# A hybrid encoder block with product-key experts: half of the last products in float32r parts, one load ahead, one load tied, the accumulator in four pieces

## The chip, the core and the metric

The kernel runs on one core of one Trainium2 chip. Its five engines are named as in the profile: PE (matrix products; PEld is its loading of weights), DVE (vector), ACT (scalar, activation functions), POOL, and SP, which here only issues DMA transfers. The metric is the device time of one execution in microseconds (us).

## The reference

`x` is 512 tokens by 1024 features in float32. One layer is computed:

```python
h = rms_norm(x, norm1_g)
q, k, v, xr, yr, gate_logits = split(h @ w_in)
attn = diff_attention(q, k, v, ...)            # 8 heads, two softmaxes each, chunk-causal
rnn = rg_lru(conv(xr), ...) * gelu(yr)         # 1280 channels
merged = sigmoid(g_A) * (attn @ P_A) + sigmoid(g_R) * (rnn @ P_R)
x = x + merged @ w_out
h = rms_norm(x, norm2_g)
# PEER: per token 8 heads pick 16 of 16384 experts each, by product keys
act = gelu(sum_d u_tab[idx] * h)               # 128 chosen rows per token
x = x + sum_k softmax(score) * act * v_tab[idx]
```

`u_tab` and `v_tab` are 16384 by 1024 in float32.

## The kernel before, in words

Tokens lie in four blocks of 128. Block 0 goes through everything up to the keys as pass 0, blocks 1 to 3 as pass 1. The experts are then computed in two ways. For blocks 0 and 1 each token's rows are gathered (`experts`, L843): 128 slots per block, in each slot an indirect DMA of POOL (L871) fetches 1 MB, a row of `u` and of `v` for each token, into one of four buffers `uv`; DVE multiplies and sums the `u` half with `h` (L883 for block 0, L857 for block 1), ACT makes the weight from it (L862, L863), and DVE adds the weighted `v` half to the output (L848).

Blocks 2 and 3 together (256 tokens) go through all experts (`dense`, L995). The tables are cut into 128 chunks of 128 experts. Each chunk c has an "up" product, `u` chunk times `h` into PSUM tile `pup` or `st`, then a gelu by ACT into `y` (L946), and a "down" product, which adds `o` times `v` chunk to an accumulator `acc` in PSUM of 256 tokens by 1024 features, held over all 128 chunks. `o` is `y` times the tokens' weights for these experts (L1060, DVE). The weights are built before (`wbuild`, L1011), written to a DRAM tensor `w_d` in 16 groups of tokens, and read back as tiles `w` for 12 chunks each (L1048).

47 up products are made ahead. The other 81 (`up_near`) are made between the down products, from chunk 32 on: each has its `u` chunk loaded as `raw`, cast by ACT to float32r (L926), and the rest of the cast taken by DVE (L927); the two parts are the tile `t`. Such a product with both factors in parts is three float32r products, high by high, high by low and low by high (`mm`, L207). A down product is plain float32: 4 calls of 128x128 by 128x512, each of which the profile shows as two MATMUL instructions, so 8 in all.

The slots of block 1 (`second`, L1125) are let go step by step beside the dense part: 0.6 of a slot for each down product alone, 1.1 where an up product goes with it (`share`).

Every engine takes its instructions in one order, which a scheduler sets when the kernel is built. A `v` load brings two chunks (1 MB). `v` and `t` tiles share four buffers of 8 KB, `raw` has three, `o` three. SP issues the loads in its own order, and one that waits holds back those behind it. `tc.add_manual_dep(..., in_turn)` ties an instruction behind another.

The change touches the head (L117, L395 to L398), `dense` (L997, L1000, the tie at L1048 and L1056, the down product L1050 to L1065) and its end (L1091 to L1095).

Of the kernel before, what the change touches and what calls it, by code (L numbers as in the profile page):

```python
# [10 lines left out]
F32 = mybir.dt.float32  # L11
F32R = mybir.dt.float32r
# [51 lines left out]
def block_kernel(  # L64
# [23 lines left out]
    uvp = ctx.enter_context(tc.tile_pool(name="uvp", bufs=4))  # L88
# [3 lines left out]
    wp = ctx.enter_context(tc.tile_pool(name="wp", bufs=4))  # L92
    rg = ctx.enter_context(tc.tile_pool(name="rg", bufs=5))
# [97 lines left out]
    x1_d = dram.tile([3, P, D], F32, name="x1_d")  # L191
# [7 lines left out]
    def rstd_of(ss, w, scale):  # L199
        xx = small(w)  # L200
        nc.gpsimd.tensor_scalar(xx, ss, scale, EPS, op0=ALU.mult, op1=ALU.add)  # L201
        y = small(w)
        nc.gpsimd.tensor_tensor(y, xx, mhalf[:, 0:w], op=ALU.pow)
        return y


    def mm(o, lhs, rhs, start, stop):  # L207
        terms = [(0, 0)] if len(lhs) == 1 or len(rhs) == 1 else [(0, 0), (0, 1), (1, 0)]
        made = [
            nc.tensor.matmul(  # L210
                o, lhs[a], rhs[b], start=start and i == 0, stop=stop and i == len(terms) - 1
            )
            for i, (a, b) in enumerate(terms)
        ]
        return made[0]


    in_turn = mybir.DependencyInfo(mybir.DependencyClass.Sync, mybir.DependencyReason.SCHED_ONLY)
# [129 lines left out]
    class Pass:  # L348
# [43 lines left out]
            return [h[:, k, :] for h in self.hT]  # L392


        def head(self):  # L395
            nb, NT = self.nb, self.NT
            xt = self.region([P, nb, D])
            nc.sync.dma_start(xt, x[self.t0 : self.t0 + NT, :].rearrange("(b p) d -> p b d", p=P))  # L398
            self.hT = self.parts()
            for b in range(nb):  # L400
                hh = s4.tile([P, D], F32, tag="s4", name=nm("hh"))
                ss = small(1)
                A.activation(hh, xt[:, b, :], AF.Square, accum_out=ss)  # L403
                rs = rstd_of(ss, 1, 1.0 / D)
                A.activation(hh, xt[:, b, :], AF.Copy, scale=rs[:, 0:1])
                for k in range(0, KT, 4):
                    pt = psum("pth")
                    for j in range(4):
                        nc.tensor.transpose(pt[:, j * P : (j + 1) * P], hh[:, (k + j) * P : (k + j + 1) * P], ident)
                    for j in range(4):  # L410
                        g1 = cst[:, C_N1 + k + j : C_N1 + k + j + 1]
                        o = self.hT[0][:, k + j, b * P : (b + 1) * P]
                        pj = pt[:, j * P : (j + 1) * P]
                        A.activation(o, pj, AF.Copy, scale=g1)
                        if self.split:
                            V.scalar_tensor_tensor(
                                self.hT[1][:, k + j, b * P : (b + 1) * P], pj, g1, o.bitcast(F32),
                                op0=ALU.mult, op1=ALU.subtract,
                            )
# [484 lines left out]
    NT2 = 2 * P  # L904
    TG = 16
    NG = NT2 // TG
    NCH = SLOTS
# [8 lines left out]

    WI = 12

    w_d = dram.tile([NG, P, NCH, TG], F32, name="w_d")

    def chunk(src, c, name):
# [41 lines left out]
    turn, owed = [None], [0.0]  # L963
    SHARE = {"far": 0.2, "w": 0.5, "down": 0.6, "both": 1.1}

    def share(step):
        owed[0] += SHARE[step]
        while owed[0] >= 1:
            owed[0] -= 1
            next(ex, None)  # L970
# [23 lines left out]

    def dense(ys, kT, kTb, stack):  # L995
        pool = lambda n, bufs=1, **kw: stack.enter_context(tc.tile_pool(name=n, bufs=bufs, reuse_waits="tile", **kw))
        dw = pool("dw")  # L997
        pa = pool("pa", space=PSUM)
        pt_ = pool("pt", 2, space=PSUM)
        acc = pa.tile([P, 2, D], F32, tag="acc", name="acc")  # L1000

        def up_near(after=None):
            c = TURN[len(ys)]
# [35 lines left out]
        ws, vs = [], []  # L1039

        def wtile():
            n = min(WI, NCH - len(ws) * WI)
            ws.append(rg.tile([P, NG, n, TG], F32, tag="r", name=nm("w")))

        def wload(j, g0=0, g1=NG):
            i1, w = j * WI, ws[j]
            n = w.shape[2]
            nc.sync.dma_start(w[:, g0:g1], w_d[g0:g1, :, i1 : i1 + n, :].rearrange("g p i t -> p g i t"))  # L1048

        def down(c, y):  # L1050
            if c % WI == 0 and len(ws) * WI < NCH:
                wtile()
                wload(len(ws) - 1)
            if c % 2 == 0:
                vs.append(wp.tile([P, 2, D], F32, tag="w8", name=nm("v")))
                nc.sync.dma_start(vs[-1], v_t[c : c + 2].rearrange("c p d -> p c d"))  # L1056
            v_ = vs[-1][:, c % 2, :]
            o = mid.tile([P, NT2], F32, tag="o", name=nm("o"), bufs=OB)
            yv = y.rearrange("p (g t) -> p g t", g=NG)
            turn[0] = V.tensor_mul(o.rearrange("p (g t) -> p g t", g=NG), yv, ws[c // WI][:, :, c % WI, :])  # L1060
            for b in range(2):
                bs = slice(b * P, (b + 1) * P)
                for hf in range(2):
                    hs = slice(hf * 512, hf * 512 + 512)
                    mm(acc[:, b, hs], [o[:, bs]], [v_[:, hs]], c == 0, c == NCH - 1)  # L1065

        for tg in range(NG):
            last = wbuild(tg)
# [6 lines left out]
                wload(0, 0, 8)  # L1075
            elif tg == 13:
                wload(0, 8, 14)
        wload(0, 14, NG)
        while len(ys) < AHEAD:
            up_near(last)  # L1080

        A.copy(h2s[0], p1.h2r)
        V.tensor_tensor(h2s[1], p1.h2r, h2s[0].bitcast(F32), op=ALU.subtract)
        for c in range(NCH):
            down(c, ys[c])

            more = c >= HEAD + SPARE and len(ys) < NCH
            if more:
                up_near()
            share("both" if more else "down")  # L1090
        for b in range(2):  # L1091
            ob = wp.tile([P, D], F32, tag="raw", name=nm("ob"), bufs=3)
            nc.sync.dma_start(ob, x1_d[1 + b])
            V.tensor_add(ob, ob, acc[:, b, :])
            nc.sync.dma_start(out[(2 + b) * P : (3 + b) * P, :], ob)  # L1095

    p0, p1 = Pass(0, 1, False), Pass(1, 3, True)
    st = {}
    p0.head()
    run(p0.qkv(0, st))  # L1100
    attend(p0, st)
    run(p0.rnn())
# [37 lines left out]
    with ExitStack() as stack:  # L1140
        dense(ys, *kTs, stack)
# [83 lines left out]
```

## Time and profile before

| | |
|---|---|
| median of 3 runs | 1873.72 us (1872.7 to 1874.15) |
| the profiled execution's own time | 1872.16 us |
| its span, first to last instruction | 1870.4 us |
| mean granted TensorE clock | 0.956 of full speed |
| busy, PE / PEld / DVE / ACT / POOL | 93% / 73% / 70% / 42% / 27% of the span |
| chain that ended last | PE 73%, DMA 10%, DVE 8%, ACT 4%, issue 4%, POOL 2% |
| read from HBM, written | 539.68 MB, 22.02 MB (300 GB/s over the span) |

How to read it: times in the trace are counted from the span's start. A stretch given as A:B is from A to B us. "DMA share" is the mean busy share of the core's 16 DMA engines. Matmuls are pipelined and their ends modelled, so the mean duration of one overlaps its neighbours; the time that a run of them takes is read from the chain. The granted clock is 1.00 where PE runs at 2.4 GHz. The dense part's down products lie from about 1185 to 1864 us.

### The profile page before, as it was taken

How to read it: one execution, taken by the hardware profiler on the slowest of the kernel's cores; microseconds unless marked ns; L12 is line 12 of the kernel's file. 1: busy time of each engine (PE TensorE's matmuls, PEld its weight loads, DVE VectorE, ACT ScalarE, POOL GpSimd, SP SyncE). 2: the span in 40 equal slices, each digit the busy share in tenths (PEclk: the TensorE clock that was granted, in tenths of full speed). 3: DMA queues.
4: the chain of work that ended last, by engine and by line, in shares of the span. 5: the costliest groups of instructions: out<-in, count | busy, mean ns of one | idle time of the engine just before them, and what ended most of it. 6: DMA issues, size and time to landing. Idle time of an engine off the chain costs nothing.

```text
span 1870.4 us, 25606 instructions
## 1 busy us (share of the span) xinstructions
PE 1739.8 (93%) x9102; PEld 1366.9 (73%) x9102; DVE 1303.3 (70%) x2811; ACT 780.0 (42%) x2188; POOL 498.4 (27%) x375
## 2 busy tenths in 40 slices
PE   7899898889969899998999987899999999999998
PEld 6689797778849677778988976444767667766763
DVE  2251287999999987679999787345766666766663
ACT  3382334676678754345411576001222233222220
POOL 1100001544342233332000477121322232222220
PEclk9899898889869899998999999999999999999999
DMA  7478554887878899988566677999999999999894
GB/s 302 146 273 312 187 184 158 301 310 259 328 274 306 325 360 360 380 313 304 169 195 222 207 273 304 365 389 341 401 358 377 380 370 371 342 363 361 336 357 186
DMA packets 131471, 563.37 MB, mean 301 GB/s; under 512 B 11408, under 2 KB 43280, under 8 KB 88592
## 3 DMA queue, kind: packets, MB, share of 16 engines
q1 hardware_dynamic: 94480, 293.29, 43.2%
q0 software_dynamic: 36864, 268.45, 38.1%
q8 instruction: 72, 1.18, 0.2%
q14 instruction: 55, 0.45, 0.1%
HBM read 539.68 MB, written 22.02 MB: 300 GB/s over the span
## 4 chain that ended last, share of the span: by engine, by line
PE 73%; DMA 10%; DVE 8%; ACT 4%; issue 4%; POOL 2%; DVEq 0%; SPq 0%; POOLq 0%; ACTq 0%
PE acc L210 22%; PE st L210 15%; PE pup L210 5%; PE ppq L210 5%; DMA uv<-in_uv_dram,idx 5%; PE pgt L210 4%; PE pkq L210 4%; PE pbR L690 4%; PE pbA L683 3%; PE pwo L717 3%; DMA v<-in_v_t_dram 2%; DVE x1f L848 2%; PE pvv L210 2%; PE pw L1034 1%; DVE uv L883 1%
## 5 line engine op out<-in xcount | busy, mean ns | idle before, releaser
L871 POOL DMA_INDIRECT uv<-in_uv_dram,idx x256 | 362.7, 1417 | 1074.1 <-DVE x1g L848 265.5
L210 PE MATMUL acc<-v,o 128*128 128x512 f32 x1024 | 448.8, 594 | 4.4 <-DMA v<-in_v_t_dram 4.4
L210 PEld LDWEIGHTS acc<-v,o 128*128 128x128 f32 x1024 | 191.8, 190 | 230.1 <-issue 223.3
L210 PE MATMUL st<-h2s,t 128*128 128x256 f32 x1944 | 252.6, 288 | 0.0
L210 PEld LDWEIGHTS st<-h2s,t 128*128 128x128 f32 x1944 | 235.0, 188 | 20.1 <-issue 17.2
L848 DVE SCALAR_TENSOR_TENSOR x1g<-uv,e,x1g 128x1024 f32<-128x1024 f32 x128 | 164.3, 1284 | 47.5 <-ACT e L863 47.4
L848 DVE SCALAR_TENSOR_TENSOR x1f<-uv,e,x1f 128x1024 f32<-128x1024 f32 x128 | 163.7, 1279 | 18.4 <-ACT e L894 18.3
L883 DVE SCALAR_TENSOR_TENSOR uv<-uv,h2f 128x1024 f32<-128x1024 f32 x128 | 155.6, 1217 | 29.3 <-DMA uv<-in_uv_dram,idx 28.3
L862 ACT ACTIVATE e<-e 128x1 f32<-128x1 f32 x128 | 25.9, 202 | 335.9 <-DVE uv L857 335.2
L857 DVE SCALAR_TENSOR_TENSOR uv<-uv,h2g 128x1024 f32<-128x1024 f32 x128 | 156.4, 1222 | 10.7 <-DMA uv<-in_uv_dram,idx 5.7
L927 DVE TENSOR_TENSOR t<-raw,t 128x1024 fp32r<-128x1024 f32 x81 | 99.0, 1222 | 69.3 <-ACT t L926 69.3
L210 PE MATMUL pup<-r,u 128*128 128x256 f32 x496 | 107.6, 379 | 0.3 <-DMA u<-in_u_t_dram 0.3
L234 DVE TENSOR_TENSOR wl<-raw,wh 128x1024 fp32r<-128x1024 f32 x76 | 90.9, 1217 | 21.1 <-PE pgt L210 10.1
L946 ACT ACTIVATE y<-st 128x256 f32<-128x256 f32 x81 | 31.1, 384 | 176.1 <-PE st L210 176.1
L210 PEld LDWEIGHTS pup<-r,u 128*128 128x128 f32 x496 | 93.9, 190 | 13.4 <-issue 0.8
L1060 DVE TENSOR_TENSOR o<-y,w 128x256 f32<-128x256 f32 x96 | 40.6, 423 | 90.3 <-PE acc L210 90.1
L926 ACT CAST t<-raw 128x1024 fp32r<-128x1024 f32 x81 | 83.8, 1034 | 23.4 <-PE acc L210 23.4
L233 ACT CAST wh<-raw 128x1024 fp32r<-128x1024 f32 x76 | 76.7, 1044 | 30.1 <-PE pwo L717 11.2
L1034 PE MATMUL pw<-o1s,o 128*128 128x128 f32 x512 | 66.8, 285 | 18.8 <-ACT wst L1035 8.9
L1033 POOL TENSOR_SCALAR o1s<-iota,r 128x128 f32<-128x128 bf16 x64 | 80.5, 1266 | 10.0 <-issue 4.2
L1034 PEld LDWEIGHTS pw<-o1s,o 128*128 128x128 f32 x512 | 62.6, 196 | 23.4 <-ACT wst L1035 10.5
L201 POOL TENSOR_SCALAR sm<-sm 128x1 f32<-128x1 f32 (+4 forms) x24 | 9.6, 398 | 253.6 <-ACT hh L403 111.5
(271 smaller groups left out, 3340.6 us busy)
## 6 DMA issues: line engine op xcount, KB each, us to landing
v<-in_v_t_dram SPq DMA_DIRECT2D x64, 1024.0 KB, 9.2
raw<-in_u_t_dram SPq DMA_DIRECT2D x81, 512.0 KB, 8.7
u<-in_u_t_dram SPq DMA_DIRECT2D x47, 512.0 KB, 4.0
w<-in_w_br_dram SPq DMA_DIRECT2D x16, 1024.0 KB, 5.0
w_d<-wst SPq DMA_DIRECT2D x16, 1024.0 KB, 5.1
w<-w_d SPq DMA_DIRECT2D x9, 1536.0 KB, 14.0
w<-in_w_qkv_dram SPq DMA_DIRECT2D x12, 1024.0 KB, 6.8
raw<-in_w_qkv_dram SPq DMA_DIRECT2D x24, 512.0 KB, 6.2
```

The lines of the kernel that those rows point to most:

```text
L210: nc.tensor.matmul(o, lhs[a], rhs[b], start=start and i == 0, stop=stop and i == len(terms) - 1)
L233: A.copy(hi[:, i : i + 1024], raw)
L234: V.tensor_tensor(lo[:, i : i + 1024], raw, hi[:, i : i + 1024].bitcast(F32), op=ALU.subtract)
L690: nc.tensor.matmul(pb[:, 0:NT], w.raw(1024 + k * P, 1024 + (k + 1) * P), self.rnn_out(k, 1)[:, 0, :], start=(k == 0), stop=(k == NF - 1),)
L848: V.scalar_tensor_tensor(x1, v_, e_, x1, op0=ALU.mult, op1=ALU.add)
L857: i = V.scalar_tensor_tensor(t[:, 0:D], t[:, 0:D], 1.0, h2, op0=ALU.mult, op1=ALU.mult, accum_out=d)
L871: i = nc.gpsimd.indirect_dma_start(out=t, out_offset=None, in_=uv, in_offset=bass.IndirectOffsetOnAxis(ap=idx[:, s : s + 1], axis=0),)
L883: i = V.scalar_tensor_tensor(t[:, 0:D], t[:, 0:D], 1.0, h2, op0=ALU.mult, op1=ALU.mult, accum_out=d)
L926: A.copy(t[:, 0, :], raw)
L927: V.tensor_tensor(t[:, 1, :], raw, t[:, 0, :].bitcast(F32), op=ALU.subtract)
L1033: e.tensor_scalar(o1, iota, k1, g1, op0=ALU.is_equal, op1=ALU.mult)
L1034: last = nc.tensor.matmul(pw[:, j, :], o2[:, j, :], o1, start=True, stop=True)
```

## The change

1. The first block of `x` is loaded into a tile of its own ahead of the constants, and given to `head`.
2. In `down`, odd chunks, and all chunks from 114 (`LATE`) on, have `v` and `o` cast to float32r by ACT, and the rests taken by DVE; the product is made of three float32r products. Even chunks below 114 stay as they were. The parts are held in tiles `vhl`, `ohi` and `olo`. `vhl` of an odd chunk, `ohi` and `olo` have one buffer each, in a pool `sp` that takes the place of the pool `dw`, which is closed once the weights are built; `vhl` of an even chunk takes one of the five buffers `r`.
3. The third `v` load (chunks 4 and 5) is tied behind the load of the last two groups of `w` (`whole`).
4. `acc` is four tiles of 128 by 512 in place of one of 128 by 2 by 1024; at the end each is added and written out by itself.

```diff
+    x0 = uvp.tile([P, 1, D], F32, tag="uv", name="x0")
+    nc.sync.dma_start(x0, x[0:P, :].rearrange("(b p) d -> p b d", p=P))
     nc.sync.dma_start(cst, consts)
...
-        def head(self):
+        def head(self, xt=None):
             nb, NT = self.nb, self.NT
-            xt = self.region([P, nb, D])
-            nc.sync.dma_start(xt, x[self.t0 : self.t0 + NT, :].rearrange("(b p) d -> p b d", p=P))
+            if xt is None:
+                xt = self.region([P, nb, D])
+                nc.sync.dma_start(xt, x[self.t0 : self.t0 + NT, :].rearrange("(b p) d -> p b d", p=P))
...
+    LATE = 114
...
-        dw = pool("dw")
+        building = stack.enter_context(ExitStack())
+        dw = building.enter_context(tc.tile_pool(name="dw", bufs=1, reuse_waits="tile"))
...
-        acc = pa.tile([P, 2, D], F32, tag="acc", name="acc")
+        acc = [[pa.tile([P, 512], F32, tag=f"acc{b}{h}", name=nm("acc")) for h in range(2)] for b in range(2)]
...
-                nc.sync.dma_start(vs[-1], v_t[c : c + 2].rearrange("c p d -> p c d"))
+                i = nc.sync.dma_start(vs[-1], v_t[c : c + 2].rearrange("c p d -> p c d"))
+                if c == 4:
+                    tc.add_manual_dep(i.ins, whole.ins.name, in_turn, reason="in turn")
...
+            lhs, rhs = [o], [v_]
+            if c % 2 or c >= LATE:
+                vhl = (sp if c % 2 else rg).tile([P, 2, D], F32R, tag="vhl" if c % 2 else "r", name=nm("vhl"))
+                vhi, vlo = vhl[:, 0, :], vhl[:, 1, :]
+                A.copy(vhi, v_)
+                V.tensor_tensor(vlo, v_, vhi.bitcast(F32), op=ALU.subtract)
+                ohi = sp.tile([P, NT2], F32R, tag="ohi", name=nm("ohi"))
+                A.copy(ohi, o)
+                olo = sp.tile([P, NT2], F32R, tag="olo", name=nm("olo"))
+                V.tensor_tensor(olo, o, ohi.bitcast(F32), op=ALU.subtract)
+                lhs, rhs = [ohi, olo], [vhi, vlo]
             for b in range(2):
                 bs = slice(b * P, (b + 1) * P)
                 for hf in range(2):
                     hs = slice(hf * 512, hf * 512 + 512)
-                    mm(acc[:, b, hs], [o[:, bs]], [v_[:, hs]], c == 0, c == NCH - 1)
+                    mm(acc[b][hf], [t[:, bs] for t in lhs], [t[:, hs] for t in rhs], c == 0, c == NCH - 1)
...
-        wload(0, 14, NG)
+        whole = wload(0, 14, NG)
...
+        building.close()
+        sp = pool("sp")
...
+        for b in range(2):
+            for h in range(2):
+                hs = slice(h * 512, h * 512 + 512)
+                V.tensor_add(obs[b][:, hs], obs[b][:, hs], acc[b][h])
+                nc.sync.dma_start(out[(2 + b) * P : (3 + b) * P, hs], obs[b][:, hs])
...
-    p0.head()
+    p0.head(x0)
```

The order on SP around the third `v` load, before. The `v` rows are the loads of chunks 0 and 1, 2 and 3, 4 and 5, 6 and 7; the `u` rows are the last chunks of the up products made ahead; `128x2x192` is the `w` load of the last two groups.

```order
L1056 DMA v_2131_10584<-in_v_t_dram 128x2x1024
L1056 DMA v_2136_10605<-in_v_t_dram 128x2x1024
L1036 DMA w_d_172<-wst_2103_10442 128x2048
L1056 DMA v_2141_10626<-in_v_t_dram 128x2x1024
L935 DMA u_2125_10545<-in_u_t_dram 128x1024
L935 DMA u_2127_10557<-in_u_t_dram 128x1024
L1048 DMA w_1993_9980<-w_d_172 128x2x192
L935 DMA u_2129_10569<-in_u_t_dram 128x1024
L1048 DMA w_2130_10582<-w_d_172 128x16x192
L1056 DMA v_2146_10647<-in_v_t_dram 128x2x1024
```

The same place on SP now:

```order
L1063 DMA v_2134_10591<-in_v_t_dram 128x2x1024
L1063 DMA v_2142_10627<-in_v_t_dram 128x2x1024
L1043 DMA w_d_174<-wst_2106_10445 128x2048
L940 DMA u_2128_10548<-in_u_t_dram 128x1024
L940 DMA u_2130_10560<-in_u_t_dram 128x1024
L1055 DMA w_1996_9983<-w_d_174 128x2x192
L940 DMA u_2132_10572<-in_u_t_dram 128x1024
L1055 DMA w_2133_10589<-w_d_174 128x16x192
L1063 DMA v_2150_10663<-in_v_t_dram 128x2x1024
L1063 DMA v_2158_10699<-in_v_t_dram 128x2x1024
```

The third `v` load went from ahead of the last three `u` loads and both `w` loads to behind them.

The order on DVE in the stage where up and down products alternate, near chunk 96, before. `t` is the rest of a `u` chunk's cast, `o` the left factor of a down product, `uv,e` a slot's product with `h`, `x1g` its addition.

```order
L927 TENSOR_TENSOR t_2721_13954<-raw_2720_13952,t_2721_13954 128x1024
L857 SCALAR_TENSOR_TENSOR uv_2707_13889,e_2708_13891<-uv_2707_13889,h2g_8977 128x1024
L1060 TENSOR_TENSOR o_2725_13990<-y_2613_13326,w_2623_13380 128x256
L927 TENSOR_TENSOR t_2728_13999<-raw_2727_13997,t_2728_13999 128x1024
L848 SCALAR_TENSOR_TENSOR x1g_8976<-uv_2707_13889,e_2708_13891,x1g_8976 128x1024
L1060 TENSOR_TENSOR o_2735_14044<-y_2620_13371,w_2623_13380 128x256
L857 SCALAR_TENSOR_TENSOR uv_2714_13934,e_2715_13936<-uv_2714_13934,h2g_8977 128x1024
L848 SCALAR_TENSOR_TENSOR x1g_8976<-uv_2714_13934,e_2715_13936,x1g_8976 128x1024
```

The same place on DVE now, for the same pair of up products (`vhl` is the low part of a `v` chunk, `olo` of an `o`):

```order
L1077 TENSOR_TENSOR vhl_2854_14610<-v_2845_14561,vhl_2854_14610 128x1024
L932 TENSOR_TENSOR t_2868_14681<-raw_2867_14679,t_2868_14681 128x1024
L1070 TENSOR_TENSOR o_2885_14786<-y_2749_14008,w_2752_14017 128x256
L860 SCALAR_TENSOR_TENSOR uv_2851_14601,e_2852_14603<-uv_2851_14601,h2g_8977 128x1024
L851 SCALAR_TENSOR_TENSOR x1g_8976<-uv_2851_14601,e_2852_14603,x1g_8976 128x1024
L1081 TENSOR_TENSOR olo_2875_14724<-o_2872_14717,ohi_2874_14722 128x256
L860 SCALAR_TENSOR_TENSOR uv_2861_14661,e_2862_14663<-uv_2861_14661,h2g_8977 128x1024
L1070 TENSOR_TENSOR o_2892_14831<-y_2758_14057,w_2752_14017 128x256
L932 TENSOR_TENSOR t_2878_14741<-raw_2877_14739,t_2878_14741 128x1024
L851 SCALAR_TENSOR_TENSOR x1g_8976<-uv_2861_14661,e_2862_14663,x1g_8976 128x1024
```

Two instructions per pair are new, and the second `t` now stands behind `olo` of the next pair. So it stands in 15 of the stage's 41 pairs; in most others the second `t` is ahead of `olo`. On ACT, too, the second `t` cast of this pair is now behind the `ohi` cast.

The order on DVE in the last chunks, from the row for the low part of chunk 114 on (all chunks in parts):

```order
L1077 TENSOR_TENSOR vhl_3029_15621<-v_3027_15617,vhl_3029_15621 128x1024
L1081 TENSOR_TENSOR olo_3031_15626<-o_3028_15619,ohi_3030_15624 128x256
L1077 TENSOR_TENSOR vhl_3033_15642<-v_3027_15617,vhl_3033_15642 128x1024
L1070 TENSOR_TENSOR o_3043_15691<-y_2925_15036,w_2863_14668 128x256
L1077 TENSOR_TENSOR vhl_3040_15672<-v_3038_15668,vhl_3040_15672 128x1024
L1081 TENSOR_TENSOR olo_3035_15647<-o_3032_15640,ohi_3034_15645 128x256
L1070 TENSOR_TENSOR o_3050_15721<-y_2935_15096,w_2863_14668 128x256
L1077 TENSOR_TENSOR vhl_3051_15723<-v_3049_15719,vhl_3051_15723 128x1024
L1081 TENSOR_TENSOR olo_3042_15677<-o_3039_15670,ohi_3041_15675 128x256
L1077 TENSOR_TENSOR vhl_3044_15693<-v_3038_15668,vhl_3044_15693 128x1024
L1070 TENSOR_TENSOR o_3056_15749<-y_2943_15143,w_2863_14668 128x256
L860 SCALAR_TENSOR_TENSOR uv_3036_15661,e_3037_15663<-uv_3036_15661,h2g_8977 128x1024
```

Before, DVE had one `o` for a chunk here, and the slots' two instructions at every second chunk or so; now each chunk has `o`, `vhl` and `olo`. The eight slots left at chunk 114 are spread over the same rows.

## Rows read from the trace of the kernel before

**Rows 1.** Busy time by stretch; columns: engines' busy us (instructions), clock, DMA share, GB/s

```profile
1184.00:1308.00 124.00, 119.63 (x304) 56.08 (x303) 55.74 (x85) 11.31 (x38) 24.96 (x19) 0.99 0.96 363
1200.00:1280.00 80.00, 78.50 (x184) 34.59 (x183) 37.97 (x59) 5.96 (x24) 18.46 (x13) 1.00 1.03 390
1308.00:1600.00 292.00, 292.00 (x1501) 203.24 (x1500) 199.30 (x252) 86.39 (x201) 80.92 (x53) 1.00 0.98 377
1600.00:1806.00 206.00, 206.00 (x1040) 141.66 (x1039) 136.72 (x173) 58.63 (x137) 54.76 (x36) 1.00 0.92 351
1806.00:1863.70 57.70, 57.70 (x153) 26.83 (x151) 26.31 (x39) 4.25 (x17) 7.18 (x6) 1.00 0.63 232
```

**Rows 2.** The chain that ended last; columns: start us, us, what, instructions

```profile
776.23 8.32 PE pgt L210 x48
...
1448.62 6.87 PE acc L210 x16
1455.48 5.65 PE st L210 x48
...
1808.86 54.95 PE acc L210 x128
```

**Rows 3.** Groups of DVE and ACT, 1308 to 1806; busy us, mean ns, idle before

```profile
L848 DVE SCALAR_TENSOR_TENSOR x1g<-uv,e,x1g 128x1024 f32<-128x1024 f32 x89 | 114.0, 1280 | 35.8 <-ACT e L863 35.8
L857 DVE SCALAR_TENSOR_TENSOR uv<-uv,h2g 128x1024 f32<-128x1024 f32 x89 | 108.4, 1218 | 0.0
L927 DVE TENSOR_TENSOR t<-raw,t 128x1024 fp32r<-128x1024 f32 x79 | 96.6, 1222 | 68.0 <-ACT t L926 68.0
L926 ACT CAST t<-raw 128x1024 fp32r<-128x1024 f32 x79 | 81.7, 1034 | 14.5 <-PE acc L210 14.5
L946 ACT ACTIVATE y<-st 128x256 f32<-128x256 f32 x80 | 30.7, 384 | 173.2 <-PE st L210 173.2
L1060 DVE TENSOR_TENSOR o<-y,w 128x256 f32<-128x256 f32 x71 | 30.0, 422 | 52.1 <-PE acc L210 51.8
L863 ACT ACTIVATE e<-e,g 128x1 f32<-128x1 f32 x89 | 26.1, 293 | 2.0
L862 ACT ACTIVATE e<-e 128x1 f32<-128x1 f32 x89 | 18.0, 202 | 165.3 <-DVE uv L857 164.7
```

**Rows 4.** What DVE waited for, 1308 to 1806; us in total, times, longest us

```profile
DVE t L927 <- ACT t L926: 68.0, 52, 4.2
DVE o L1060 <- PE acc L210: 57.4, 41, 3.0
DVE x1g L848 <- ACT e L863: 35.8, 37, 4.5
```

**Rows 5.** What PE waited for, 1184 to 1300; us in total, times, longest us

```profile
PE acc L210 <- DMA v<-in_v_t_dram: 4.4, 2, 2.9
```

**Rows 6.** Timeline around the third v load; columns: start us, us, engine, line, operation

```profile
1160.99 0.37 SPq L1056 DMA_DIRECT2D v<-in_v_t_dram  x1
1162.10 3.79 SPq L935 DMA_DIRECT2D u<-in_u_t_dram  x2
...
1176.13 9.32 PE L210 MATMUL st<-r,u 128*128 128x256 f32 x32 [7.15 <-DMA u<-in_u_t_dram]
1177.88 1.10 DVE L1060 TENSOR_TENSOR o<-ys,w 128x256 f32<-128x256 f32 x3 [15.49 <-DMA w<-w_d]
```

**Rows 7.** Timeline of the start

```profile
0.73 0.39 SPq L117 DMA_DIRECT2D cst<-in_consts_dram  x1
...
1.65 0.42 SPq L398 DMA_DIRECT2D r<-in_x_dram  x1
...
5.59 1.06 ACT L403 ACTIVATE hh<-r 128x1024 f32<-128x1024 f32 x1 [1.15 <-DMA r<-in_x_dram]
```

**Rows 8.** Timeline of the end

```profile
1863.83 2.35 DVE L1094 TENSOR_TENSOR ob<-ob,acc 128x1024 f32<-128x1024 f32 x2 [9.88 <-PE acc L210]
1865.08 1.47 SPq L1095 DMA_DIRECT2D out_dram<-ob  x2
```

More of the change, by code (lines that the diff above doesn't have):

```diff
@@ L1047, in wload @@
             n = w.shape[2]
-            nc.sync.dma_start(w[:, g0:g1], w_d[g0:g1, :, i1 : i1 + n, :].rearrange("g p i t -> p g i t"))
+            return nc.sync.dma_start(w[:, g0:g1], w_d[g0:g1, :, i1 : i1 + n, :].rearrange("g p i t -> p g i t"))
         def down(c, y):
@@ L1090, in dense @@
             share("both" if more else "down")
+        obs = []
         for b in range(2):
[L1092 to L1095, printed above, removed]
+            obs.append(wp.tile([P, D], F32, tag="raw", name=nm("ob"), bufs=3))
+            nc.sync.dma_start(obs[b], x1_d[1 + b])
+        for b in range(2):
[3 more added lines that the diff above has]
+                nc.sync.dma_start(out[(2 + b) * P : (3 + b) * P, hs], obs[b][:, hs])
     p0, p1 = Pass(0, 1, False), Pass(1, 3, True)
     st = {}
-    p0.head()
+    p0.head(x0)
     run(p0.qkv(0, st))
```

## The prediction

> **What bounds the kernel now.** I read the busy times by stretch first, then the chain, then the groups and waits of DVE, and last the timelines of the places that the change touches. The part that changes lies from 1184 on, and PE bounds it: from 1308 to 1863.7 PE is busy in every microsecond, at the full clock [rows 1]. The chain there is PE alone, 16 `acc` instructions in 6.87 us (two chunks), then 48 `st` instructions in 5.65 us (two up products), over and over: 12.52 us for a pair [rows 2]. At the end 128 `acc` instructions follow each other in 54.95 us [rows 2]. Two others stand close behind. The transfers fill the DMA engines to 0.98 at 377 GB/s from 1308 to 1600, and to 1.03 at 390 GB/s from 1200 to 1280, where PE also waits 4.4 us for `v` [rows 1, 5]. DVE is busy 199.3 of 292 us and 136.7 of 206 us, two thirds [rows 1], and most of its other third goes in waits: 68.0 us for the cast of `t`, 57.4 for PE, 35.8 for the slot's weight [rows 4].
>
> **What a product in parts saves on PE.** A chunk in float32 takes 8 instructions of 6.87/16 = 0.429 us, 3.43 us. In parts it takes 12 float32r instructions of 512 columns, which the trace does not show. It shows 256 columns at 5.65/48 = 0.118 us and 384 at 8.32/48 = 0.173 us [rows 2]; the line through both gives 0.229 at 512. Bounds: half of a float32 instruction, 0.215, and twice the 256 columns, 0.235. I take the line: 12 x 0.229 = 2.75 us, 0.69 less per chunk (0.61 to 0.86). In parts are 16 odd chunks before the up products, 41 beside them and the 14 from 114 on, 71 x 0.69 = 49 us on PE.
>
> The Trainium skill ("TensorE: Matmul & The Clock Gate", the section "Wait — 56ns, not 53.3ns?") gives 215.7 ns for 512 columns at the full clock, columns over 2.4 GHz and about 2.5 ns: by that a chunk saves 0.85 and all 60 us. The trace agrees for float32, 0.429 being twice 0.2133 and 2.8 ns, but not for float32r, where the same rule would make 256 columns 109 ns and the row shows 118.
>
> **What it costs on DVE and ACT, and in which stage.** Each such chunk adds on ACT a cast of 128x1024 (1.03 us, as `t`) and one of 128x256 (0.38, as `y`), and on DVE a difference of 128x1024 (1.22) and one of 128x256 (0.42, as `o`) [rows 3]. For a pair DVE has 199.3 x 12.52/292 = 8.55 us now and 10.2 then, of 11.83. It still fits, but in one order, and the single buffers decide.
>
> I walked one pair through the new orders. Time 0 is the start of the even chunk. The odd one ends at 6.18 (3.43 + 2.75), the first up product at 9.0, the second at 11.83. The cast `ohi` of the next pair has to wait until 6.18, when PE lets go of its one buffer; it ends at 6.56, and `olo` behind it on DVE at 6.98. Where the second `t` stands ahead of `olo`, it is ready by 7 and nothing waits. Where it stands behind, as in the rows shown, DVE goes on with a slot (1.22), `o` (0.42) and then `t` (1.22), and ends at 9.84, while PE wants it at 9.0: 0.84 and a signal, 0.9 us. This is so in 15 pairs. In three of them `olo` comes so late anyway that `t` is ready at 8.9; in ten it costs 0.9; in two, the addition of a slot or more stands ahead of `t` as well, and it costs about 3.4. Sum 9 + 6.8 = 15.8. The 41 chunks save 28.3, so this stage gains 12.5 us (bounds 0, where each pair loses what it gains, and 28).
>
> Do the transfers allow it? From 1308 to 1600 they are 292 us x 377 GB/s = 110 MB; at 390 they need 282 us, so up to 10 us can go there; from 1600 to 1806, at 351 GB/s, some 20 could. The 12.5 is about 7 and 5.5 of these, and fits.
>
> **Chunks 0 to 32.** The 16 odd chunks take 11 us off PE. The third `v` load (1 MB, 2.7 us at 390 GB/s) goes from ahead of the `u` loads to behind them: it was issued at 1160.99, the `u` loads followed at 1162.10, and PE stood 7.15 us for them until 1176.13, DVE 15.49 for `w` [rows 6]. So up to 2.7 us come off that wait; what is late next is the third `v` itself, needed four chunks (14 us) after the first begins. But the stretch is bound by transfers: 124 us x 363 GB/s need 115 us at 390 [rows 1], so at most 9 of the 14 us can be had, and with the even chunk's share of `v` let go earlier (after its cast and its even product) some are. I take 5 (0 to 9).
>
> **Chunks 114 to 127.** All are in parts, and `ohi` and `olo` have one buffer: the cast can only begin when PE is through with the chunk before, so PE stands about 0.5 us (0.38 and two signals) in each chunk, and 2.75 becomes 3.25. DVE has `o`, `vhl` and `olo`, 2.06 us per chunk, and the five slots that stand behind chunk 114's rows, 2.5 each: 41 us of 46. Walked through, it is late by about 0.1 in each chunk: 3.38 against 3.43, 0.7 us gained. Bounds: 9.7 gained if the casts hide; 4 lost if the signals take 0.3 us more each.
>
> **Start and end.** `x` was issued 0.92 us after the constants, 1.65 against 0.73, and landed for ACT at 5.59, which begins the chain [rows 7]: 0.9 gained. At the end two additions take 2.35 us and the writes follow [rows 8]; in four pieces only the last, half of one, 0.6 us, stands behind the last product, and the last write is half as long: 2 us gained (1.2 to 2.5).
>
> **Sum.** 0.9 + 5 + 12.5 + 0.7 + 2 = 21.1 us off the profiled execution's 1872.16: 1851. The median of the runs is 1.6 above that execution, so I predict 1852.5.
>
> **The rivals.** (a) PE gets the whole of it: the scheduler's order is loose enough that DVE and ACT run ahead. For it: 57.4 us of DVE's waits are for PE, slack that a shorter product takes up [rows 4]. Against it: the single buffers. Then 28.3 + 9 + 9.7 + 2.9 = 50 us, 1824. (b) The transfers hold the stretch to 1600: its 0.98 share is all there is, and the mix with up products cannot go beyond 377 GB/s. Against it: 390 a little earlier [rows 1]. Then only the stage from 1600 gains, 5.5, and 0.7 + 2.9 with it, and 2 of the first stretch: 11 us, 1863.
>
> The Trainium skill ("DMA: Bandwidth & Descriptors", the section "Where 436 GB/s comes from") puts the bound of one core's HBM traffic at about 358 GB/s and that of the fabric at 435. By the first, the stretch from 1308 to 1600 would be beyond its bound now and the change worth nothing there, which is (b); by the second there would be room for all of (a). The trace shows 377 and 390, so the first does not hold here, and the second is not shown.
>
> (c) Slower: DVE becomes the bound from 1308 on. Its waits for ACT do not shrink when it gets busier, as they come from its order: (68.0 + 35.8) us in 39.8 pairs, 2.6 for a pair [rows 4]. With 10.2 busy that is 12.8 us, 0.3 more than the pair takes now, 41 x 0.3 = 12 us lost, and each of the two new differences also waits for a cast of ACT: if one of them waits as `t` does on average, 68.0/79 = 0.86, 41 x 1.15 = 47 lost. It decides from the point where busy and waits together pass 12.52, so a wait of 0.3 in the pair brings no gain and each 0.1 more costs 4 us. I price it near its low end, 12 lost, 5 gained elsewhere: 1881.
>
> **How the numbers follow.** The forecast 0.45 (1838 to 1860), (a) 0.14, (b) 0.2, (c) 0.13, and 0.08 that gains and losses cancel. A measurement tells 0.2%, 3.7 us, from no change. Faster: 0.45 + 0.14 + 0.2, and little of the rest, 0.8; within 0.2% 0.07; slower 0.13. The range for 8 in 10 reaches from 1830, leaving out most of (a), to 1876, leaving out most of (c).
>
> **What would show it.** In the profile after: 12 float32r `acc` instructions in 2.75 us, 48 `st` still in 5.65; waits of PE `st` for DVE `t` (or of weights), about 16 us in all and near 0.9 each, where `t` stands behind `olo`; DVE `olo` waiting for ACT `ohi` and ACT `ohi` for PE `acc`; from chunk 114 on a wait of 0.5 before each chunk; transfers near 390 GB/s until 1600; PE's wait for `u` near 1170 at 4.5 in place of 7.15. The prediction is wrong if float32r instructions take over 0.28 us, if DVE's busy share passes 0.95 in the stage, or if PE waits there for transfers of `u` or `v`.

## The result and the profile after

The changed kernel takes 1853.35 us (median of 5 runs, 1849.23 to 1854.64), the kernel before 1874.15 beside it (1872.7 to 1877.4): a ratio of 0.9877 (0.9861 to 0.9894), 20.8 us faster. Forecast were 1852.5 in 1830 to 1876. The profiled execution took 1853.35, its span 1851.6.

The total came out within 1 us, which is in part luck: two of its terms were off by 6 us each, in opposite directions (5.9 forecast for the start and chunks 0 to 32 together, 0.2 lost; 0.7 forecast for the last chunks, 6.8 gained). Between the two profiled executions 18.8 us went, where 21.1 were forecast. To see it, the program is cut where PE starts the first instruction of chunks 0, 32 and 114 of the down products. "Work" is the count of PE's instructions in a piece times 0.429 us (float32, 512 columns), 0.229 (float32r, 512) or 0.118 (float32r, 256); "lost" is the rest, waits and slow instructions. Figures are rounded, so a sum can miss by 0.1.

| piece | before: us = work + lost | after: us = work + lost | moved | forecast |
|---|---|---|---|---|
| up to chunk 0 | 1185.3 | 1182.8 | -2.5 | -0.9, and up to -2.7 by the tie |
| chunks 0 to 32 | 122.8 = 114.8 + 8.0 | 125.4 = 108.3 + 17.2 | +2.7 | with the tie -5 |
| chunks 32 to 114 | 507.5 = 507.5 + 0 | 496.5 = 475.0 + 21.5 | -11.1 | -12.5 |
| 114 to the last product | 48.2 = 48.1 + 0.1 | 41.5 = 38.5 + 3.0 | -6.8 | -0.7 |
| from there to the span's end | 6.6 | 5.4 | -1.2 | -2 |

The two middle pieces cannot be laid side by side as they stand. In the changed kernel 38 more `st` instructions, 4.5 us, lie ahead of chunk 32 (79, and 41 before). Like for like, chunks 0 to 32 became 1.8 us shorter and chunks 32 to 114 became 6.6 us shorter.

Busy time by stretch in the changed kernel, to be laid beside [rows 1] (columns as there):

```profile
1184.00:1308.00 124.00, 114.07 (x396) 72.42 (x395) 76.31 (x111) 31.69 (x66) 22.47 (x17) 0.94 0.97 366
1240.00:1250.00 10.00, 6.04 (x7) 2.52 (x8) 4.70 (x5) 1.54 (x3) 1.34 (x2) 0.50 1.03 411
1240.00:1260.00 20.00, 16.04 (x42) 9.09 (x43) 9.97 (x14) 4.01 (x9) 2.81 (x3) 0.75 0.97 379
1308.00:1580.00 272.00, 261.87 (x1468) 205.88 (x1467) 219.97 (x283) 108.06 (x234) 83.45 (x50) 0.99 0.99 380
1554.00:1560.00 6.00, 5.98 (x25) 4.80 (x26) 5.40 (x6) 1.76 (x4) 1.68 (x1) 0.74 0.94 354
1580.00:1790.00 210.00, 205.70 (x1176) 162.88 (x1175) 175.56 (x223) 86.40 (x184) 59.07 (x40) 1.00 0.98 373
1790.00:1846.00 56.00, 54.59 (x231) 40.57 (x229) 49.91 (x72) 26.37 (x49) 7.66 (x5) 1.00 0.67 255
```

Before, PE was never idle from 1308 on; now it is idle 10 of 272 us to 1580, and DVE has risen from two thirds to four fifths. Two stretches show a granted clock near 0.75, and in both PE had just waited: 7.1 us until 1243.96, and 1.6 and 2.2 us, the second until 1554.02. From 1240 to 1250 the clock was 0.50, the lower of its two levels (1.2 GHz). The chain of the changed kernel, beside [rows 2]:

```profile
1540.74 6.20 PE acc L212 x20
1546.93 2.84 PE st L212 x24
1554.02 4.01 PE st L212 x20
...
1594.35 6.18 PE acc L212 x20
1600.53 5.65 PE st L212 x48
1606.18 6.18 PE acc L212 x20
```

A pair of chunks takes 6.18 (8 instructions of 0.429 and 12 of 0.229, so 2.75), two up products still 5.65. The second and third rows belong to one pair of up products that was broken up: its 48 instructions took until 1558.03, 11.1 us, with two waits for `t` in between. What PE waited for from 1150 to 1850:

```profile
PE st L212 <- DVE t L932: 11.3, 14, 2.2
PE acc L212 <- DMA v<-in_v_t_dram: 7.8, 2, 7.1
PE st L212 <- DMA u<-in_u_t_dram: 5.3, 1, 5.3
PE st L212 <- ACT t L931: 4.5, 3, 1.6
...
PE acc L212 <- DVE olo L1081: 0.5, 1, 0.5
PE acc L212 <- ACT ohi L1079: 0.5, 2, 0.3
```

The `st` waits for `t` are 11.3 + 4.5 = 15.8 us in this window. 2.2 of them lie ahead of chunk 32; the stage that the prediction walked through has 13.7, in 15 waits at 13 places, where 15.8 were forecast. The wait for `u` fell from 7.15 [rows 6] to 5.3. New is 7.1 us for one `v`; before, PE waited 4.4 in two [rows 5]. DVE's waits from 1308 to 1800, beside [rows 4]:

```profile
DVE x1g L851 <- ACT e L866: 27.2, 49, 1.5
DVE t L932 <- ACT t L931: 26.0, 27, 1.8
DVE o L1070 <- PE acc L212: 14.8, 14, 1.8
DVE olo L1081 <- ACT ohi L1079: 11.0, 11, 3.6
DVE vhl L1077 <- ACT vhl L1076: 9.6, 9, 3.9
```

DVE's waits for ACT were 68.0 + 35.8 [rows 4]; with two kinds of casts more they are 73.8. The third rival rested on their staying as they were.

### The profile page after: what moved, and what is told of

Its sections match the earlier page's. It is cut to its first block, busy times and chain, and to the rows that moved or that the text cites. A ratio compares the mean times of both kernels' runs of the same rounds, so it can differ in the third digit from the quotient of the medians.

```text
span 1851.6 us, 26537 instructions
## 1 busy us (share of the span) xinstructions
PE 1702.7 (92%) x9386; PEld 1421.3 (77%) x9386; DVE 1408.8 (76%) x2955; ACT 872.5 (47%) x2330; POOL 506.9 (27%) x375
## 4 chain that ended last, share of the span: by engine, by line
PE 55%; DVE 12%; issue 11%; DMA 10%; ACT 7%; POOL 3%; SPq 0%; DVEq 0%; POOLq 0%; ACTq 0%
PE acc L212 16%; PE st L212 13%; DMA uv<-in_uv_dram,idx 6%; PE pup L212 5%; PE ppq L212 5%; PE pkq L212 5%; POOL uv L874 3%; DVE x1f L851 2%; DMA v<-in_v_t_dram 2%; DVE uv L886 1%; PE pw L1041 1%; DVE t L932 1%; PE pgt L212 1%; PE pvv L212 1%; DVE wl L236 1%
## 5 line engine op out<-in xcount | busy, mean ns | idle before, releaser
L874 POOL DMA_INDIRECT uv<-in_uv_dram,idx x256 | 373.9, 1461 | 1051.7 <-DVE x1g L851 399.2
L212 PE MATMUL st<-h2s,t 128*128 128x256 f32 x1944 | 247.4, 283 | 15.8 <-DVE t L932 11.3
L212 PEld LDWEIGHTS st<-h2s,t 128*128 128x128 f32 x1944 | 240.4, 189 | 25.8 <-DVE t L932 14.2
L212 PE MATMUL acc<-v,o 128*128 128x512 f32 x456 | 208.7, 601 | 7.8 <-DMA v<-in_v_t_dram 7.8
L212 PE MATMUL acc<-vhl,ohi 128*128 128x512 f32 x568 | 192.9, 429 | 1.5 <-ACT ohi L1079 0.5
L851 DVE SCALAR_TENSOR_TENSOR x1f<-uv,e,x1f 128x1024 f32<-128x1024 f32 x128 | 163.7, 1279 | 17.7 <-ACT e L897 17.6
L860 DVE SCALAR_TENSOR_TENSOR uv<-uv,h2g 128x1024 f32<-128x1024 f32 x128 | 156.8, 1225 | 16.2 <-DMA uv<-in_uv_dram,idx 16.2
L212 PEld LDWEIGHTS acc<-v,o 128*128 128x128 f32 x456 | 84.6, 193 | 93.0 <-issue 83.3
L212 PEld LDWEIGHTS acc<-vhl,ohi 128*128 128x128 f32 x568 | 106.2, 188 | 47.4 <-issue 23.7
L212 PE MATMUL acc<-vhl,olo 128*128 128x512 f32 x284 | 104.6, 392 | 0.7 <-DVE olo L1081 0.5
L1077 DVE TENSOR_TENSOR vhl<-v,vhl 128x1024 fp32r<-128x1024 f32 x71 | 86.6, 1220 | 19.9 <-ACT vhl L1076 19.5
## 6 DMA issues: line engine op xcount, KB each, us to landing
w<-w_d SPq DMA_DIRECT2D x9, 1536.0 KB, 17.7
```

Source lines behind the costliest of these rows:

```text
L212: nc.tensor.matmul(o, lhs[a], rhs[b], start=start and i == 0, stop=stop and i == len(terms) - 1)
L851: V.scalar_tensor_tensor(x1, v_, e_, x1, op0=ALU.mult, op1=ALU.add)
L860: i = V.scalar_tensor_tensor(t[:, 0:D], t[:, 0:D], 1.0, h2, op0=ALU.mult, op1=ALU.mult, accum_out=d)
L874: i = nc.gpsimd.indirect_dma_start(out=t, out_offset=None, in_=uv, in_offset=bass.IndirectOffsetOnAxis(ap=idx[:, s : s + 1], axis=0),)
L1077: V.tensor_tensor(vlo, v_, vhi.bitcast(F32), op=ALU.subtract)
```

## The experiments

Each kernel ran with the kernel before on the same chip. Runs of one kernel spread by up to 16 us here (the kernel before from 1866.9 to 1883.3 beside e9 to e11; e10 from 1866.4 to 1880.3), so a difference of under 5 us between kernels of different sets is not read as one. The pieces below come from one profiled execution each, cut as above; those of e2, e6 and e7 were the fastest of their kernels, 5.8, 6.9 and 4.3 us below the median, and that of e11 lies 5.3 above it. The number of `st` instructions ahead of chunk 32 also differs, by 0.118 us each: 49 in e1, e2, e4 and e6, 79 in e3 and e7, 88 in e5, 51 in e8, 23 in e9. And chunk 0 begins between 1176.7 and 1185.2 in eleven kernels with the same start and the same tie (all but e7, without the tie, and e12, with other slots ahead), so its place is not read as the work of either.

| kernel | us (median) | ratio to before, 95% | chunk 0 at | 0 to 32 | 32 to 114 | 114 to end | rest |
|---|---|---|---|---|---|---|---|
| e1_no_parts | 1869.6 | 0.9957 (0.9941-0.9972) | 1184.5 | 123.0 | 506.5 | 48.2 | 4.0 |
| e2_mid | 1856.7 | 0.9900 (0.9878-0.9922) | 1180.2 | 122.9 | 493.8 | 48.2 | 4.0 |
| e3_early | 1872.6 | 0.9981 (0.9965-0.9997) | 1180.7 | 125.4 | 512.6 | 48.2 | 4.0 |
| e4_late | 1864.1 | 0.9934 (0.9915-0.9953) | 1185.2 | 122.9 | 506.1 | 42.6 | 5.4 |
| e5_two_ohi | 1847.4 | 0.9843 (0.9819-0.9868) | 1183.5 | 118.9 | 494.8 | 42.8 | 5.4 |
| e6_no_early | 1855.2 | 0.9885 (0.9867-0.9904) | 1180.0 | 124.3 | 495.4 | 41.5 | 5.4 |
| e7_no_tie | 1856.4 | 0.9897 (0.9877-0.9917) | 1182.5 | 122.6 | 497.2 | 42.3 | 5.7 |
| e8_half_gathers | 1841.4 | 0.9803 (0.9780-0.9827) | 1183.6 | 106.6 | 503.3 | 41.4 | 5.4 |
| e9_half_gathers_no_early | 1861.7 | 0.9930 (0.9902-0.9958) | 1182.4 | 114.2 | 519.5 | 41.8 | 5.4 |
| e10_late56 | 1872.8 | 0.9994 (0.9972-1.0017) | 1176.7 | 119.5 | 524.2 | 42.3 | 6.5 |
| e11_vlo_pool | 1905.7 | 1.0161 (1.0128-1.0193) | 1183.9 | 130.3 | 516.2 | 65.1 | 13.8 |
| e12_ahead | 1854.3 | 0.9874 (0.9847-0.9902) | 1199.7 | 112.5 | 492.7 | 42.8 | 5.4 |

**One part at a time.** Four kernels of one set, which differ in one line (the first also leaves out the pool that the parts would lie in):

```
-            if c % 2 or c >= LATE:
+            if False:                        # e1_no_parts
+            if c % 2 and 32 < c < LATE:      # e2_mid
+            if c % 2 and c <= 32:            # e3_early
+            if c >= LATE:                    # e4_late
```

> No product in parts; x ahead, the tied v load and the four pieces stay. Theory (stage by stage, with the first stretch held by its transfers): 1.15 at the start, 1.85 of the wait for u, 1.2 at the end, so about 1870 (4.2 below before), and chunk 0 to chunk 32 takes the 122.7 us of before. Rival (the tie makes the third v late, and that ate the gain of the first stretch): chunk 0 to 32 takes 125 to 126 and the time is 1872 to 1873.

> Parts for the 41 odd chunks beside the up products alone. Theory: the 4.2 of the kernel without parts and about 11 of this stage: 1859; chunk 32 to 114 about 11 us shorter than before. Rival (PE's time is given back elsewhere, as transfers set the end): 1865 or more.

> Parts for the 16 odd chunks up to 32 alone, 11 us less work on PE. Theory (transfers hold that stretch): nothing beyond the 4.2, 1870 (1868 to 1873), chunk 0 to 32 in 122 to 126 us. Rival (PE bounds it and something else in the changed kernel ate it): chunk 0 to 32 in 113 to 117 us and 1861 to 1863.

> Parts for chunks 114 to 127 alone. Theory (the cast hides under the last products of the chunk before): 2.96 us per chunk, 4.2 + 6.8 below before: 1863. Rival (the prediction's bubble of 0.5 per chunk, and the gain seen there came from earlier stages): 3.3 to 3.4 per chunk and 1869.

The theory held in all four times. The head, the tie and the four pieces bring 6.2 (1875.8 to 1869.6; forecast 0.9, up to 2.7, and 2). Against that kernel, parts beside the up products bring 12.9 (forecast 12.5), parts in the last chunks 5.5 (forecast 0.7), and parts in chunks 0 to 32 alone lose 3.0. Together 21.6, and the whole change 20.8: within the spread, the parts add up.

Not all that the early parts lose is lost where they stand. In e3_early the stage behind chunk 32 has no product in parts, and still 9.5 us are lost there, where e1_no_parts loses nothing. Of these 5.1 are waits for `t`, the first of them in chunk 35:

```profile
1330.96 0.51 PE L212 MATMUL st<-h2s,t 128*128 128x256 f32 x2 [1.41 <-ACT t L931]
```

So the stages are not independent: the early parts bring waits behind chunk 32 as well.

**What holds chunks 0 to 32.** Every second slot let go there works on the rows of the one before it; in the second kernel the early products are whole again as well.

```
+            if not (table and 14 <= s < 34 and s % 2):
+                t = uvp.tile(...); ...indirect_dma_start(out=t, ...)
-            if c % 2 or c >= LATE:                      # e9 alone
+            if c % 2 and c > 32 or c >= LATE:
```

> Every second gather of the slots let go in chunks 0 to 32 is left out (ten slots work on the rows of the slot before them; DVE, ACT and PE keep all their instructions). About 10 MB less of transfers, 26 us at 390 GB/s. Theory (transfers hold that stretch): the wait of chunk 16 for v and its half-speed chunk go, of the 17.2 us lost from chunk 0 to 32 under 8 stay, chunk 32 is 9 or more earlier, and the time is 1836 to 1845. Rival (v waits for its buffer, which vhl and vlo hold): the wait stays above 5 and chunk 0 to 32 above 121.

> The ten gathers left out as in e8_half_gathers, and no parts in the odd chunks up to 32. Theory (with the transfers out of the way PE bounds the stretch, and the early parts are worth their 11 us): chunk 0 to 32 takes 114 to 118 in place of 106.6, and the time is 1848 to 1853. Rival (early parts are worth nothing whatever the transfers): chunk 0 to 32 under 110 and 1840 to 1844.

With 10 MB less to move, PE does not wait once from chunk 0 to 32, in either kernel. The busy time there in e8_half_gathers, columns as above:

```profile
1200.00:1280.00 80.00, 80.00 (x269) 49.19 (x268) 64.97 (x96) 25.53 (x55) 12.44 (x8) 1.00 0.95 354
```

DVE and ACT of e8 have as many instructions as in the changed kernel, and `vhl` has the same buffers, so it was the transfers and not a buffer that `vhl` holds. PE's order did change with it (51 `st` instructions ahead of chunk 32 and not 79), which accounts for 3.3 us of the 18.8 that the stretch became shorter. And then the early parts pay: 106.6 against 114.2 without them, and that with 28 more `st` instructions in the stretch, so the whole 11 us. The time of e9 missed its expectation by 8 us or more: its stage from 32 to 114 took 16 us longer than that of e8. 3.3 of them are those `st` instructions, 7.1 are longer waits of PE (23.3 and 16.2), and most of the rest goes with the granted clock, 0.96 from 1310 to 1580 where e8 has 0.98. Why PE waits longer is open.

**The tie and the early parts undone, one each.**

```
-                if c == 4:
+                if c == -1:                             # e7_no_tie
-            if c % 2 or c >= LATE:
+            if c % 2 and c > 32 or c >= LATE:           # e6_no_early
```

> The changed kernel with the third v load not tied. Theory of the prediction (the third v takes 2.7 us ahead of u): PE's wait for u is 7.1 instead of 5.3, chunk 0 begins about 2 us later, and the time is 1854 to 1856. Rival (transfers are the bound to chunk 32 in either order, so what u gains v loses): the wait of chunk 16 for v is shorter by as much, and the time is that of the changed kernel, 1853.

> As the changed kernel, without parts in the 16 odd chunks up to 32. Theory (there transfers are the bound and parts bring a longer wait for v and a half-speed chunk behind it): chunk 0 to 32 in 123 instead of 125.4, chunk 32 to 114 in 494 instead of 496.5: 1848 (1845 to 1851), faster than the changed kernel. Rival (the early parts do gain, and what was lost was lost elsewhere): 1855 to 1860.

Without the tie PE stands 8.8 us for `u` instead of 5.3, and 5.4 for `v` instead of 7.8; chunk 0 begins at the same time. What `u` gains `v` loses, and the two times cannot be told apart. Without the early parts the profiled pieces are 2.2 us shorter from chunk 0 on, but that is the kernel's fastest run, and the median is no better than that of the changed kernel: the expected 1848 did not come. By the ratios, 0.9885 and 0.9877, the early parts are worth nothing, to within some 5 us either way.

**What delays `t`.** Two changes were to take away PE's waits for it.

```
-OB = 3
+OB = 2                                                  # e5_two_ohi
-                ohi = sp.tile([P, NT2], F32R, tag="ohi", name=nm("ohi"))
+                ohi = sp.tile([P, NT2], F32R, tag="ohi", name=nm("ohi"), bufs=2)

-                V.tensor_tensor(vlo, v_, vhi.bitcast(F32), op=ALU.subtract)
+                nc.gpsimd.tensor_tensor(vlo, v_, vhi.bitcast(F32), op=ALU.subtract)   # e11_vlo_pool
```

> Two buffers for ohi (one of the three of o given up for its room). Theory (the one buffer of ohi holds back olo, and olo holds back t on DVE): of PE's 13.7 us of st waits from 1306 on, less than 5 stay, and the 3.0 us lost in chunks 114 to 127 fall under 1: 1843 (1840 to 1847). Rival (the waits come from where t stands in DVE's order, whatever the buffers): the waits stay above 10 and the time is 1851 to 1856.

> The low part of v, 1.22 us on DVE for each product in parts, is made on POOL, which waits for slots in two thirds of that stage. Theory (PE's 14 us of waits for t come from the number of instructions that stand in DVE's order ahead of t): under 7 of them stay, and the time is 1845 to 1850. Rival (a POOL instruction of that size is several times longer and shares DVE's port, so the gathers and the release of v come late): PE waits for v, and the time is 1858 or more.

Both theories failed. With two `ohi`, PE still waited 12.9 us for DVE's `t` and 1.5 for ACT's, and 20.9 were lost from 32 to 114; the rival's time, 1851 or more, did not come either. DVE's waits from 1308 to 1800 in that kernel say why the buffer alone is no help:

```profile
DVE olo L1081 <- PE acc L212: 24.2, 22, 2.6
```

`olo` has one buffer too, and takes the place of `ohi`. The kernel also gives up one of three `o` for the room, and no run parts the two edits. Its 1847.4 is the lowest time of a kernel that computes the whole reference; the gain lies in chunks 0 to 32, where 9.6 us were lost instead of 17.2, and PE waited 4.9 for `v` instead of 7.8; why `v` came earlier is open. In e11_vlo_pool the rival was right, but that PE waited for `vhl` and `olo` more than for `v`. On POOL the difference takes twice what it takes on DVE, and DVE stands still for much of that time:

```profile
L1077 POOL TENSOR_TENSOR vhl<-v,vhl 128x1024 fp32r<-128x1024 f32 x38 | 93.7, 2466 | 16.4 <-ACT vhl L1076 10.1 <-issue 5.9
```

```profile
1385.06 3.96 DVE L932 TENSOR_TENSOR t<-raw,t 128x1024 fp32r<-128x1024 f32 x1
1385.58 2.35 POOL L1077 TENSOR_TENSOR vhl<-v,vhl 128x1024 fp32r<-128x1024 f32 x1
```

This `t` takes 3.96 us instead of 1.22 and ends 1.1 behind POOL's instruction. So it is with 58 instructions of DVE beside the 71 differences on POOL: they took up to 6.3 us, 101 us more in all than their like in the changed kernel. PE's waits for `t` from 32 to 114 rose from 13.7 to 22.5. The last gather was issued 63 us behind the start of chunk 114 and not 18, and from there on the kernel lost 23.6 us more. So the edit freed DVE of 71 differences, 87 us, and cost it 101, and the run tells nothing of what less work on DVE would bring.

**More parts, and earlier gathers.**

```
-    LATE = 114
+    LATE = 56                                           # e10_late56
-    SHARE = {"far": 0.2, "w": 0.5, "down": 0.6, "both": 1.1}
+    SHARE = {"far": 0.35, "w": 0.5, "down": 0.48, "both": 1.1}   # e12_ahead, on e5_two_ohi
```

> Every chunk from 56 on in parts, so 29 more even ones: 20 us less work on PE, and for a pair of chunks 1.64 us more on DVE, 11.8 busy where PE needs 11.1. Theory (DVE then bounds the stage, and its waits for ACT's casts come on top, as in the prediction's third rival): a pair takes 12.5 to 13.2 and the time is 1866 to 1885, slower than the changed kernel. Rival (DVE's waits shrink to nothing as it fills): a pair takes 11.8 and the time is 1845 to 1848.

> As e5_two_ohi (1847.4), with the slots paced so that about four more gathers start before chunk 0, where the transfers fill 0.61 to 0.73 of the DMA engines, and about four fewer in chunks 0 to 32, where they fill them. Theory (each of the ten gathers left out in e8_half_gathers brought 1.2 us): chunk 0 to 32 in 115 instead of 118.9, and 1843 (1839 to 1847). Rival (DVE is busy in all of 940 to 1020, so four slots of 2.5 us there hold back the picks, and with them chunk 0, by up to 10): chunk 0 begins at 1188 or later and the time is 1850 to 1858.

From chunk 84 to 112, where all three kernels issue the same 648 `st` instructions, the 14 pairs take 172.5 us before, 167.2 in the changed kernel, and 184.4, 13.2 for a pair, with every chunk in parts. The whole gain is gone. From 1480 to 1790, first the changed kernel, then this one:

```profile
1480.00:1790.00 310.00, 300.02 (x1701) 237.52 (x1700) 256.45 (x327) 125.57 (x269) 89.47 (x59) 0.99 0.98 375
```

```profile
1480.00:1790.00 310.00, 282.92 (x1717) 250.35 (x1718) 272.14 (x352) 149.25 (x298) 95.60 (x54) 0.97 0.96 358
```

DVE goes from 83% to 88% busy, and PE from 97 to 91; in this stretch PE waits 12.8 us for ACT's half of `t`, 8.5 for DVE's and 5.4 for ACT's half of `vhl`. A pair takes what the theory gave, but not for its reason: DVE's waits for ACT, which were to stay, are 64.6 us in this stretch before, 41.7 in the changed kernel and 18.4 here, and 17.7 are new, for PE to let go of `olo`. That points to the chain of casts through ACT and DVE with their single buffers as the bound, before DVE is full; this is argued and not shown. In e12_ahead both theory and rival were right in part: chunks 0 to 32 and 32 to 114 are 8.5 us shorter than in e5_two_ohi, and chunk 0 begins 16 later, behind a new wait on the way to the picks:

```profile
PE pt L959 <- DVE r L326: 10.8, 2, 6.1
```

## Why the prediction was right, and where it was not

**The product in parts: right.** The line through 256 and 384 columns gave 0.229 at 512 and 2.75 per chunk; the chain shows 6.18 for a pair, 3.43 + 2.75. The rule of the Trainium skill ("TensorE: Matmul & The Clock Gate", the section "Wait — 56ns, not 53.3ns?"), 215.7 ns for 512 columns, is not borne out for float32r.

**The stage with up products: the waits right, the gain not.** The walk (the prediction's pair of chunks, followed through the new orders) had `olo` behind the end of the odd product, then a slot, `o`, and `t`, and 0.9 us of waiting, in most of the 15 pairs. Such a place, PE, DVE and ACT of the changed kernel (columns as in [rows 6]):

```profile
1510.04 0.41 ACT L1079 CAST ohi<-o 128x256 fp32r<-128x256 f32 x1 [0.20 <-PE acc L212]
1510.06 3.23 PE L212 MATMUL st<-h2s,t 128*128 128x256 f32 x26
1510.35 1.04 ACT L931 CAST t<-raw 128x1024 fp32r<-128x1024 f32 x1
1511.07 0.42 DVE L1081 TENSOR_TENSOR olo<-o,ohi 128x256 fp32r<-128x256 f32 x1
1511.41 1.22 DVE L860 SCALAR_TENSOR_TENSOR uv<-uv,h2g 128x1024 f32<-128x1024 f32 x1
...
1512.55 0.42 DVE L1070 TENSOR_TENSOR o<-y,w 128x256 f32<-128x256 f32 x1
1512.89 1.22 DVE L932 TENSOR_TENSOR t<-raw,t 128x1024 fp32r<-128x1024 f32 x1
...
1514.16 1.10 PE L212 MATMUL st<-h2s,t 128*128 128x256 f32 x7 [0.87 <-DVE t L932]
```

`t`'s cast was over at 1511.39; ahead of its DVE half stand a slot and `o`. PE waits at 13 places for 13.7 us: 0.7 on average at eleven of them (forecast 0.9 at ten), and 2.3 and 3.8 at two, where ACT's half of `t` was late as well (forecast 3.4 at two, from slots ahead of `t` on DVE). That bears the walk out in the main. That another order would give the waits back was not shown, since the kernel with `t` ahead was not run, and the buffer of `ohi`, which the walk blamed, is only one of two.

But 21.5 us are lost there, 7.0 more than all waits of over 0.1 us (14.4), and so the stage gained 6.6 like for like where 12.5 were forecast. The starts of the instructions show where they go. The 26 `st` instructions from 1510.06 on, at 0.118 each, would let the next begin at 1513.12; it begins at 1514.16, 1.04 later, of which the profile counts 0.87 as waiting, and the first instruction behind the wait takes 0.11 longer. Some 0.27 for each of 17 waits is 4.6 us; the lower clock near 1554 is 1.5 more. The prediction counted waits at their length alone. Without early parts the stage did gain what was forecast: 12.7 in e2_mid, 11.1 in e6_no_early, against e1_no_parts with the same `st` instructions. So part of what is missing goes with the early parts.

**Chunks 0 to 32: the step that failed.** "At most 9 of the 14 us can be had", from transfers at 390 GB/s, "I take 5". Of the 11 us that 16 products in parts save, the stretch kept 1.8. It lost 17.2 us instead of 8.0. The parts let PE get ahead of the transfers until it stood at chunk 16, and the wait cost more than its length:

```profile
1230.50 3.60 PE L212 MATMUL acc<-v,o 128*128 128x512 f32 x8
...
1236.46 0.39 PE L212 MATMUL acc<-vhl,olo 128*128 128x512 f32 x1
...
1243.96 6.67 PE L212 MATMUL acc<-v,o 128*128 128x512 f32 x8 [7.11 <-DMA v<-in_v_t_dram]
```

The eight instructions behind it take 6.67 us (3.60 at full speed, the end of the last one included): 7.1 and 3.1 us went, where the kernel before waits 1.5 at the same chunk, at the full clock:

```profile
1245.34 41.44 PE L210 MATMUL acc<-v,o 128*128 128x512 f32 x96 [1.50 <-DMA v<-in_v_t_dram]
```

Chunk 12 had begun 5.6 us earlier than before, chunk 16 began 1.4 earlier. Seven of the eight slow instructions start in the stretch with the clock at 0.50. So two things in the prediction failed: the share of the saving that the transfers would let through (5 of 14 taken, the tie included), and that nothing in it priced what PE does after a wait. The same sits in the stage behind, after 1.59 and 2.16 us of waiting for `t` (0.74 from 1554 to 1560); 1.50 and 0.76 near 1401 left the clock at 1.00.

**Chunks 114 to 127: a term mis-sized.** That "the cast can only begin when PE is through with the chunk before" did not hold. In all 14 chunks the scheduler put the eight instructions with `ohi` first and the four with `olo` last:

```profile
1816.27 2.11 PE L212 MATMUL acc<-vhl,ohi 128*128 128x512 f32 x8 [0.24 <-ACT ohi L1079]
...
1818.22 1.07 PE L212 MATMUL acc<-vhl,olo 128*128 128x512 f32 x4
1818.42 0.41 ACT L1079 CAST ohi<-o 128x256 fp32r<-128x256 f32 x1 [0.29 <-PE acc L212]
```

The next cast starts at 1818.42, under the last four, which take 4 x 0.229 = 0.92. It is hidden but for a signal now and then: 41.5/14 = 2.96 per chunk and not 3.38. The bound of the prediction where the casts hide, 9.7, was the nearer one to the 6.8 gained.

**Start and end.** `x` lands for ACT at 4.31 instead of 5.59 [rows 7], 1.3 us where 0.9 were forecast. At the end the four pieces bring 2.6 where the last chunk is whole (e1, 6.6 to 4.0) but only 1.2 with it in parts: the four `olo` instructions close all quarters within a microsecond, and the additions queue up.

```profile
1845.10 1.07 PE L212 MATMUL acc<-vhl,olo 128*128 128x512 f32 x4
1845.52 2.48 DVE L1122 TENSOR_TENSOR ob<-ob,acc 128x512 f32<-128x512 f32 x4 [1.55 <-PE acc L212]
```

**The rivals.** (a) failed by the 21 us lost beside the up products and the 9 more lost ahead of them. (b) was right in the first stretch and wrong behind it: from 1308 to 1580 the transfers ran at 380 GB/s at 0.99, 3 more than before, and PE waited for none there. (c) failed here, since DVE's waits for ACT shrank; in e10_late56 the loss that it feared came, but these waits shrank further.

## What to carry to other kernels

A faster product on the bounding engine pays in a stage only as far as the stage's second resource allows: look at the share of the transfers in each stretch, and leave the slow form where they are full. Price a new wait of PE with the slow instructions behind it, not with its length alone. Before work is handed from DVE to POOL, look whether DVE goes on beside it: here the two mostly ran one behind the other. When a single buffer is to cost a bubble, look which of the consumer's instructions reads it last: the order inside the product can hide the refill, or make it plain.

## What the hardware showed unexpectedly

A float32r instruction of 512 columns went on at 0.229 us beside float32 ones with no cost in the change from one to the other (6.18 for both). PE's waits cost more than their length: behind 7.1 us of waiting, eight instructions took 6.67 us instead of 3.60 (granted clock 0.50 from 1240 to 1250), behind 1.59 and 2.16 us the clock was 0.74 for six. A difference of 128x1024 takes 2.47 us on POOL, 1.22 on DVE, and 58 instructions of DVE beside it lasted until it was over and longer (one of them 3.96 us for 1.22, in e11_vlo_pool). In short stretches the transfers of one core ran at up to 411 GB/s (e8_half_gathers, 1310 to 1330), beyond the 390 that the prediction took as their bound. The Trainium skill ("DMA: Bandwidth & Descriptors", the section "Where 436 GB/s comes from") gives about 358 as the HBM limit of one core; these runs pass it.
